# The gate projection of an encoder layer: a fourth block of 768 columns in seven products, and another order at the end

## The chip, the cores and the metric

The kernel runs on one core of one Trainium2 chip. The metric is the device time of one execution in microseconds (us); the median of several runs is compared. A profile is one execution recorded by the hardware profiler. In it PE is TensorE (matmuls), PEld its weight loads, DVE is VectorE, ACT is ScalarE, POOL is GpSimd, and SP is the engine whose queue issues most DMAs.

## The reference

One encoder layer over 256 tokens (two row blocks of 128) with a model width of 4096, in float32. The part that matters here is its end, after the output projection has been added to the residual `x`:

```
x = x + concat([y_a, y_b]) @ w_out
ple  = p @ w_ple                                         # (256, 256) @ (256, 4096)
gate = sigmoid(rms_norm(x, g_ple) @ w_ple_gate)          # (256, 4096) @ (4096, 4096)
x = x + ple * gate
return rms_norm(x, g_final)
```

The rest (input projection, latent attention, dilated attention, output projection) is the same in both kernels.

## The kernel before, in words

**Matmuls in three parts.** Each float32 operand is split into a high and a low part: ACT copies `hi` in a shorter format (L115), DVE subtracts `lo = src - hi` (L116). A product is then three matmuls, hi x hi, hi x lo and lo x hi, into one PSUM bank (`mm`, L130 to L135). The left operand, 128 tokens of one row tile of 128 inner indices, is the stationary one; 256, 384, 400 or 512 weight columns stream. So the weights must be loaded and split anew for every row tile, which is the steady work of SP, ACT and DVE.

**Steps.** All weight work is a list `steps`, run in order at the end of the function (L1465 to L1503). At step i the program issues loads ahead (`fetch`, at most RAW = 4 raw tiles held), then splits ahead (`convert`, into a ring of tiles: three `wp` tiles, in the wide blocks a fourth, `B4`), then the matmuls of step i, then one round of `advance`, which lets each spawned task (a Python generator) issue its next few instructions up to its `yield`. Every engine works through its own instructions in the order in which the program issued them; semaphores order the engines among one another. The last 25 steps look further ahead.

**Seven products (class `Block`, L769).** A wide block covers 1024 columns, as two halves, for both row blocks. Two row tiles (a pair j of 16), two row blocks and two column halves make a 2 x 2 x 2 product of blocks. A plain step (`plain_step`) does one row tile as 4 products, 12 matmuls; a pair is 8 products. A fast pair (`fast_steps`) does it in seven: four steps with 1, 2, 2 and 2 products, 21 matmuls. It needs four subtractions on DVE for the weights (L820) and sums of the left operand, which `x1_sums` has made once for pairs 0 to 6 (`zs`, in the slots B0, B2, B3, B7a and B5). `weave(fast, lead, trail, 2)` writes out the order: `lead` plain steps, then fast pairs with plain steps between, then `trail` plain steps with the two embedding steps (`wide_ple`) after the second of them. `wide_mid` (L1013) combines the products after the last fast step, `wide_done` (L1025) adds the rest after the last step, applies tanh (for the sigmoid), multiplies by the embedding, adds to the residual tile `x1[c]` and takes the squares for the final norm.

**The gate projection before.** Three wide blocks (k = 0, 1, 2) cover columns 0 to 3071, with 6, 7 and 7 fast pairs. Then come plain chunks (`Chunk`, `Old` steps): columns 3072 to 3583 (c = 6, 512 wide), 3584 to 3839 (c = 7, 256 wide) and 3840 to 4095 (c = 8, 256 wide). The last is done first for row block 0 over all 32 row tiles (eight steps of four row tiles), then for row block 1 with the same split weights, which are kept (`kept`, `stay`; five of the eight steps have slots of their own, the other three stay in the ring). So row block 0 can be finished while PE still works for row block 1. `done_g` (L1073) finishes a chunk; for c = 8 it goes on into `finish(t)` (L1113): the inverse root by three Newton steps, then for each of eight column tiles a scale and an output DMA from SP.

**g_final before.** `load_g` (L969) starts two steps after the last wide block and loads one of eight pieces of 512 columns per step, from SP, into B2 and B3. `late_gains` (L1106) multiplies the finished tiles 0 to 5 by it on DVE, `done_g` does so for columns 3072 to 3839, so the last scales are plain `tensor_scalar` (DVE) or a scaled copy (ACT, every third), except for the last 256 columns.

Of the kernel before, what the change touches and what calls it, by code (L numbers as in the profile page):

```python
# [66 lines left out]
class Chunk:  # L67
# [4 lines left out]
    def __init__(self, src, nk, n, lhs, banks, done, needs=lambda j: (), per=2, ts=(0, 1), keep=None):  # L72
        self.src, self.nk, self.n, self.lhs, self.banks = src, nk, n, lhs, banks
        self.done, self.needs, self.per, self.ts, self.keep = done, needs, per, ts, keep
        self.ps = None
# [3 lines left out]
def encoder_layer(ctx: ExitStack, tc: tile.TileContext, x, p, positions, g_mix, w_in, g_q_latent, w_uq,  # L79
# [625 lines left out]
    ss1, ss2 = (stat(NT * n).rearrange("p (t c) -> p t c", t=NT) for n in (8, 9))  # L705
# [52 lines left out]
    class Step:  # L758
# [4 lines left out]
        def __init__(self, load, split, run, needs=(), frees=0):  # L763
            self.load, self.split, self.run, self.needs, self.frees, self.after = load, split, run, needs, frees, None
            self.ring, self.flag = WP, None
# [3 lines left out]
    class Block:  # L769
# [9 lines left out]
        def __init__(self, w, lhs, sums, name, order, needs, tags, tmp, ring):  # L779
            self.w, self.lhs, self.sums, self.name, self.needs, self.tmp = w, lhs, sums, name, needs, tmp  # L780
            self.ring, self.tags = ring, dict(zip(self.NAMES, tags))
            self.ps, self.left = {}, {}
            for kind, _ in order[0]:
                for m in ("M1", "M5", "M7", "M6", "M4", "M2", "M3") if kind == "fast" else ("M2", "X", "M3", "M4"):
                    self.left[m] = self.left.get(m, 0) + 1

        def product(self, m, a, b):
            first = m not in self.ps
            if first:
                self.ps[m] = bank(self.tags[m], [Q])  # L790
            self.left[m] -= 1
            mm(self.ps[m], a, b, first, self.left[m] == 0)

        def load(self, kt):
            r = wp.tile([P, 2, Q], F32, tag="raw", name=f"raw_{kt}", bufs=RAW)
# [16 lines left out]
        def fast_steps(self, j):  # L812
# [9 lines left out]
            def split1(hi, lo):  # L822
                if isinstance(self.tmp, tuple):
                    T.extend(slot(b, [2, Q]) for b in self.tmp)
                else:
                    both = slot(self.tmp, [4, Q])
# [113 lines left out]
    blocks = [(512 * c, 512) for c in range(7)] + [(3584, 256), (3840, 256)]  # L940
    FAST, WIDE = 7, 3
# [27 lines left out]
    def load_g():  # L969
        for i in range(2):  # L970
            gF.append(slot(f"B{2 + i}", [2048]))
            for n in range(0, 2048, 512):
                nc.sync.dma_start(gF[i][:, n:n + 512],
                                  g_final[2048 * i + n:2048 * i + n + 512].unsqueeze(0).to_broadcast([P, 512]))
                if i == 1 and n == 0:
                    spawn(late_gains())
                yield

    P4 = {}
    WIDE_PLE = {(0, 0): "m0", (0, 1): "m1", (1, 0): "t0", (1, 1): "t1"}  # L980

    def wide_ple(k):
# [3 lines left out]
        def step(kt):  # L986
            box = []

            def load():
                box.append(wp.tile([P, 2, Q], F32, tag="raw", name=f"raw_e{kt}", bufs=RAW))  # L990
                nc.sync.dma_start(box[0].rearrange("p a b -> p (a b)"),
                                  w_ple[kt * P:(kt + 1) * P, 1024 * k:1024 * (k + 1)])

            def run(hi, lo):
                for (t, h), tag in WIDE_PLE.items():
                    if kt == 0:
                        ps[t, h] = bank(tag, [Q])
# [5 lines left out]
            return Step(load, lambda hi, lo: split(hi, lo, box[0]), run, ["pT", ("mid", k)], 1)  # L1003

        def out():
            for at in WIDE_PLE:
                nc.scalar.activation(P4[at], ps[at], AF.Copy)
# [5 lines left out]
    def wide_mid(k, blk):  # L1013

        def task():
            e = blk.e = slot("B1", [4, Q])
# [8 lines left out]
    def wide_done(k, blk):  # L1025
        def task():
# [5 lines left out]
            for n in range(6):  # L1032
                for i, t, h, m in quarters[n:n + 1]:
                    nc.scalar.activation(e[:, i], e[:, i], AF.Tanh, scale=r1h[:, t:t + 1])
                for i, t, h, m in quarters[n - 1:n] if n else ():
                    u, xc = e[:, i], x1[2 * k + h][:, t]
                    nc.vector.scalar_tensor_tensor(u, u, 1.0, P4[t, h], op0=ALU.add, op1=ALU.mult)
                    nc.vector.tensor_tensor(xc, u, xc, op=ALU.add)
                for i, t, h, m in quarters[n - 2:n - 1] if n > 1 else ():
                    xc = x1[2 * k + h][:, t]  # L1040
                    nc.scalar.activation(e[:, i], xc, AF.Square, accum_out=ss2[:, t, 2 * k + h:2 * k + h + 1])
                yield
        return task
# [23 lines left out]
    def x_cols(lo, n, t):  # L1067
        return x1[lo // 512][:, t, lo % 512:lo % 512 + n]

    def g_cols(lo, n):  # L1070
        return gF[lo // 2048][:, lo % 2048:lo % 2048 + n]

    def done_g(c, ts=(0, 1)):  # L1073
        lo, n = blocks[c]

        def task(ps):
            if not U:
                U.extend([slot("Q0", [512]), junk])
            for t in ts:
                nc.scalar.activation(U[t][:, :n], ps[t], AF.Tanh, scale=r1h[:, t:t + 1])  # L1080
            if c < 8:
                yield
            for t in ts:
                u, xc = U[t][:, :n], x_cols(lo, n, t)
                nc.vector.scalar_tensor_tensor(u, u, 1.0, ple[c][t], op0=ALU.add, op1=ALU.mult)
                nc.vector.tensor_tensor(xc, u, xc, op=ALU.add)
            if c < 8:
                yield
            for t in ts:
                u, xc = U[t][:, :n], x_cols(lo, n, t)  # L1090
                if c < 8:
                    nc.scalar.activation(u, xc, AF.Square, accum_out=ss2[:, t, c:c + 1])
                    nc.vector.tensor_tensor(xc, xc, g_cols(lo, n), op=ALU.mult)
                else:
                    nc.vector.scalar_tensor_tensor(u, xc, 1.0, xc, op0=ALU.mult, op1=ALU.mult,
                                                   accum_out=ss2[:, t, 8:9])
            if c == 7:
                yield
                for t in range(NT):
                    nc.vector.tensor_reduce(part2[t], ss2[:, t, :8], axis=AX.X, op=ALU.add)  # L1100
                    nc.vector.tensor_scalar(part2[t], part2[t], 1.0 / DM, EPS, op0=ALU.mult, op1=ALU.add)
            if c == 8:
                yield from finish(ts[0])
        return task

    def late_gains():  # L1106
        for c in range(2 * WIDE):
            for t in range(NT):
                nc.vector.tensor_tensor(x1[c][:, t], x1[c][:, t], g_cols(512 * c, 512), op=ALU.mult)
                yield  # L1110
                yield

    def finish(t):  # L1113
        r, a, h, w = r2[:, t:t + 1], stat(1), stat(1), stat(1)
        nc.vector.tensor_scalar(a, ss2[:, t, 8:9], 1.0 / DM, part2[t], op0=ALU.mult, op1=ALU.add)
# [9 lines left out]
        for c in range(8):  # L1125
            xc = x1[c][:, t]
            if c == 7:
                nc.vector.tensor_scalar(xc[:, :256], xc[:, :256], r, None, op0=ALU.mult)
                nc.vector.scalar_tensor_tensor(xc[:, 256:], xc[:, 256:], r, g_cols(3840, 256), op0=ALU.mult,
                                               op1=ALU.mult)  # L1130
            elif c % 3 == 1:
                nc.scalar.activation(xc, xc, AF.Copy, scale=r)
            else:
                nc.vector.tensor_scalar(xc, xc, r, None, op0=ALU.mult)
            nc.sync.dma_start(out[t * P:(t + 1) * P, 512 * c:512 * (c + 1)], xc)
            if t == 0:
# [43 lines left out]
    def lay(blk, order, mid, done, ple=None, after=(), used={}):  # L1180
# [5 lines left out]
        for i, key in enumerate(shape):  # L1186
            x = next(step[key])
            x.ring = WP + list(after) if after != () and i > last else blk.ring
# [100 lines left out]
    kept = [("B1",), ("B4",), ("B5",), ("B6",), ("B7a", "T6")]  # L1289
    stay = []  # L1290

    def embed(c, lo, n, tags):
        return Chunk(cols(w_ple, lo, n), 2, n, lambda kt: (pT[0][:, 0, kt], pT[0][:, 1, kt]), tags, done_p(c),
                     lambda j: ["pT"])

    for k in range(WIDE):
        order = weave(*((range(6), 6, 4) if k == 0 else (range(7), 4, 4)), 2)
        blk = Block(w_ple_gate[:, 1024 * k:1024 * (k + 1)], lhs_x1, x1_s, "x1_sums", order,
                    lambda kt: [("x1T", kt // 4)], LAST, "B6", WP + ["B4"])
        lay(blk, order, wide_mid(k, blk), wide_done(k, blk), wide_ple(k))  # L1300
    wide_end = len(steps)
    hooks[wide_end + 2] = lambda: spawn(load_g())
    tail_banks = {6: (("m0", "m1"), ("t0", "t1")), 7: (("m2", "o"), ("s", "m3")), 8: (("m0", "m1"), ("t0", "t1"))}

    for c, (lo, n) in enumerate(blocks):
        if c < 2 * WIDE:
            continue
        w, per = cols(w_ple_gate, lo, n), 1024 // n
        small = embed(c, lo, n, tail_banks[c][1])

        def gate(done, **k):
            return Chunk(w, 32, n, lhs_x1, tail_banks[c][0], done,
                         lambda j, per=per: [("x1T", kt // 4) for kt in range(per * j, per * (j + 1))], per=per, **k)

        if c < 8:
            g = gate(done_g(c))
            half = 12 // per
            add(g, 0, half)
            add(small)
            add(g, half)  # L1320
        else:
            add(small)
            for t in range(NT):
                add(gate(done_g(c, (t,)), ts=(t,), keep=(stay, t == 0)))
# [4 lines left out]
    class Old(Step):  # L1329


        def __init__(self, i, ch, j):
            self.i, self.ch, self.j, self.ring = i, ch, j, WP
            self.needs, self.after, self.flag = ch.needs(j), None, None
            kept_before = ch.keep and not ch.keep[1]
            self.load = None if kept_before else self.fetch
            self.frees = 0 if kept_before else 1
# [189 lines left out]
```

## Time and profile before

| What | us |
|---|---|
| Runs shown (3) | 1927.67, 1927.89, 1929.81; median 1927.89 |
| Profiled execution | 1927.64 |
| Its span, first to last instruction | 1925.9 |
| PE busy | 1909.8 (99%) |
| DVE busy | 1560.8 (81%) |
| ACT busy | 1101.3 (57%) |
| POOL busy | 74.5 (4%) |
| Last matmul ends, from the span's start | 1913.63 |

The difference between the execution and its span (1.7 us) lies around the recorded instructions. Times inside the profile count from the span's start. Matmuls overlap: a matmul's own duration is longer than the distance to the next, so prices are taken from starts. In tile names of the profile numbers are left out: `m` is any of the banks m0 to m3, `B` any of several slots, `Ah` and `Al` the high and low parts of the left operand.

### The profile page before, as it was taken

What the parts mean: (1) busy time and instruction counts of PE and PEld (TensorE: products, weight loads), DVE (VectorE), ACT (ScalarE), POOL (GpSimd) and SP (SyncE); (2) the same over time, 40 slices, a digit from 0 to 9 for tenths busy, and PEclk for the clock granted to TensorE, in tenths of its full rate; (3) what the DMA queues carried; (4) which work ended last, traced back from release to release, by engine and by line L of the source; (5) the groups of instructions that cost most, each with busy time, mean ns of one, the idle gap of its engine ahead of it and who ended that gap; (6) DMA issues with size and microseconds to landing.
All of it is one profiled execution on the core that took longest, in us unless ns stands there. A gap on an engine that the chain in (4) does not pass through costs nothing.

```text
span 1925.9 us, 25586 instructions
## 1 busy us (share of the span) xinstructions
PE 1909.8 (99%) x9272; PEld 1626.7 (84%) x9272; DVE 1560.8 (81%) x2162; ACT 1101.3 (57%) x1513; POOL 74.5 (4%) x122
## 2 busy tenths in 40 slices
PE   9999999999999999999999999999999999999997
PEld 8998889998888888888888888888888888888887
DVE  7766966665999999999887778889896698989866
ACT  6555555565555555655556666555565456666643
POOL 1001011220000000000000010000000000000000
PEclk9999999999999999999999999999999999999999
DMA  7676655455666666666664456665666656566675
GB/s 251 188 187 198 196 172 144 145 150 162 188 185 209 209 217 197 209 197 196 218 197 139 135 165 218 201 215 174 230 194 217 189 184 218 186 210 204 207 220 176
DMA packets 147342, 370.59 MB, mean 192 GB/s; under 512 B 12020, under 2 KB 45904, under 8 KB 147216
## 3 DMA queue, kind: packets, MB, share of 16 engines
q1 hardware_dynamic: 145584, 363.90, 61.9%
q0 software_dynamic: 1632, 5.05, 0.7%
q8 instruction: 73, 1.20, 0.3%
q14 instruction: 53, 0.43, 0.1%
HBM read 364.72 MB, written 4.19 MB: 192 GB/s over the span
## 4 chain that ended last, share of the span: by engine, by line
PE 94%; DVE 4%; DMA 1%; issue 1%; ACT 1%; SPq 0%; DVEq 0%; ACTq 0%
PE m L134 20%; PE m L135 20%; PE m L133 20%; PE t L134 4%; PE t L135 4%; PE t L133 4%; PE s L134 3%; PE o L134 3%; PE o L135 3%; PE o L133 3%; PE s L135 3%; PE s L133 3%; DVE lo L116 1%; PE t L445 1%; DVE B L820 1%
## 5 line engine op out<-in xcount | busy, mean ns | idle before, releaser
L116 DVE TENSOR_TENSOR lo<-raw,hi 128x1024 fp32r<-128x1024 f32 (+4 forms) x497 | 549.0, 1109 | 227.6 <-ACT hi L115 225.0
L115 ACT ACTIVATE hi<-raw 128x1024 fp32r<-128x1024 f32 (+4 forms) x497 | 478.4, 967 | 365.9 <-PE m L135 181.2
L133 PE MATMUL m<-hi,Ah 128*128 128x512 f32 (+2 forms) x1130 | 429.2, 380 | 0.0
L134 PE MATMUL m<-lo,Ah 128*128 128x512 f32 (+2 forms) x1130 | 424.6, 376 | 0.9 <-DVE lo L116 0.7
L135 PE MATMUL m<-hi,Al 128*128 128x512 f32 (+2 forms) x1128 | 422.3, 374 | 0.0
L134 PEld LDWEIGHTS m<-lo,Ah 128*128 128x128 f32 x1130 | 212.9, 188 | 34.6 <-DVE lo L116 5.0
L135 PEld LDWEIGHTS m<-hi,Al 128*128 128x128 f32 x1128 | 212.3, 188 | 32.8 <-DVE Al L127 0.2
L133 PEld LDWEIGHTS m<-hi,Ah 128*128 128x128 f32 x1130 | 213.0, 188 | 30.1
L133 PE MATMUL m<-hi,B 128*128 128x512 f32 (+1 forms) x420 | 160.4, 382 | 0.0
L134 PE MATMUL m<-lo,B 128*128 128x512 f32 (+1 forms) x420 | 156.8, 373 | 0.2 <-DVE lo L116 0.2
L135 PE MATMUL m<-hi,B 128*128 128x512 f32 (+1 forms) x420 | 156.7, 373 | 0.0
L115 ACT ACTIVATE hi<-B 128x1024 fp32r<-128x1024 f32 x75 | 79.5, 1061 | 79.9 <-DVE B L820 50.3
L116 DVE TENSOR_TENSOR lo<-B,hi 128x1024 fp32r<-128x1024 f32 x75 | 91.6, 1223 | 4.1 <-ACT hi L115 1.8
L135 PEld LDWEIGHTS m<-hi,B 128*128 128x128 f32 x420 | 78.9, 188 | 11.7
L134 PEld LDWEIGHTS m<-lo,B 128*128 128x128 f32 x420 | 79.1, 188 | 11.3 <-DVE lo L116 0.9
L133 PEld LDWEIGHTS m<-hi,B 128*128 128x128 f32 x420 | 79.0, 188 | 10.6
L115 ACT ACTIVATE B<-raw 128x1024 fp32r<-128x1024 f32 (+1 forms) x66 | 60.5, 925 | 45.8 <-DMA raw<-in_w_in_dram 17.4
L820 DVE TENSOR_TENSOR B<-raw,B 128x512 f32<-128x512 f32 x126 | 86.3, 685 | 0.0
L115 ACT ACTIVATE B<-B 128x1024 fp32r<-128x1024 f32 (+1 forms) x60 | 57.4, 957 | 44.4 <-DVE B L820 22.1
L116 DVE TENSOR_TENSOR B<-raw,B 128x1024 fp32r<-128x1024 f32 (+1 forms) x66 | 69.4, 1059 | 13.5 <-ACT B L115 13.2
L116 DVE TENSOR_TENSOR T<-t,T 128x512 fp32r<-128x512 f32 (+1 forms) x65 | 44.4, 683 | 41.6 <-ACT T L115 41.2
L835 DVE TENSOR_TENSOR lo<-raw,hi 128x1024 fp32r<-128x1024 f32 x57 | 69.5, 1219 | 1.9 <-ACT hi L833 1.8
(780 smaller groups left out, 3774.3 us busy)
## 6 DMA issues: line engine op xcount, KB each, us to landing
raw<-in_w_in_dram SPq DMA_DIRECT2D x320, 512.0 KB, 4.1
raw<-in_w_out_dram SPq DMA_DIRECT2D x128, 512.0 KB, 4.4
raw<-in_w_ple_gate_dram SPq DMA_DIRECT2D x128, 512.0 KB, 4.4
raw<-in_w_in_dram SPq DMA_DIRECT2D x63, 400.0 KB, 3.7
raw<-in_w_uq_dram SPq DMA_DIRECT2D x32, 384.0 KB, 3.5
raw<-in_w_ukv_dram SPq DMA_DIRECT2D x16, 512.0 KB, 3.7
T<-in_x_dram SPq DMA_DIRECT2D x7, 512.0 KB, 6.0
T<-in_x_dram POOLq DMA_DIRECT2D x7, 512.0 KB, 8.2
```

Of the source, the lines that this page charges most:

```text
L115: nc.scalar.activation(hi, src, AF.Copy)
L116: nc.vector.tensor_tensor(lo, src, plain(hi), op=ALU.subtract)
L133: nc.tensor.matmul(ps, ah, bh, start=start, stop=False)
L134: nc.tensor.matmul(ps, ah, bl, start=False, stop=False)
L135: nc.tensor.matmul(ps, al, bh, start=False, stop=stop)
L445: nc.tensor.transpose(tp[:, k, t * P:(t + 1) * P], e[:, t, k * P:(k + 1) * P], ident)
L820: nc.vector.tensor_tensor(dst, a, b, op=ALU.subtract)
L835: nc.vector.tensor_tensor(lo, r[1], plain(hi), op=ALU.subtract)
```

## The change

Four things are done together, all of them after block 2.

1. Columns 3072 to 3839 become a fourth wide block (k = 3) with halves of 384 columns (`q`), six fast pairs in the order 1, 2, 3, 4, 0, 5 with 6 plain steps ahead and 6 behind. After its last fast step its ring is the three `wp` tiles only. Its halves cross the borders of the 512-column tiles, so `wide_done` works in pieces.
2. The last 256 columns: weight steps 0 to 3 run for row block 0 alone, steps 4 to 7 for both row blocks (row block 0 first within a step), then 0 to 3 for row block 1 with kept weights (`KEPT`, four slots).
3. g_final is multiplied in the last scale (`scalar_tensor_tensor` on DVE) for six of the eight tiles; tiles 1 and 4 (`EARLY`) are multiplied ahead of it by GpSimd and scaled by ACT. `late_gains` is gone.
4. The loads of g_final start when the fourth fast pair of block 3 has used its sums in B2 and B3 (`z used`), one per step.

```
-    FAST, WIDE = 7, 3
+    FAST, WIDE = 7, 4
...
     def load_g():
+        while "z used" not in flags:
+            yield
         for i in range(2):
             gF.append(slot(f"B{2 + i}", [2048]))
-            for n in range(0, 2048, 512):
-                nc.sync.dma_start(gF[i][:, n:n + 512], ...)
-                if i == 1 and n == 0:
-                    spawn(late_gains())
-                yield
+        for c in (1, 4, 0, 2, 3, 5, 6, 7):
+            g = g_cols(512 * c)
+            nc.sync.dma_start(g, g_final[512 * c:512 * (c + 1)].unsqueeze(0).to_broadcast([P, 512]))
+            yield
+            if c in EARLY:
+                for t in range(NT):
+                    nc.gpsimd.tensor_tensor(x1[c][:, t], x1[c][:, t], g, op=ALU.mult)
...
+    def done_last(t, ps):
+        def task():
+            u, xc = U[t][:, :256], x1[7][:, t, 256:]
+            nc.scalar.activation(u, ps[t], AF.Tanh, scale=r1h[:, t:t + 1])
+            nc.vector.scalar_tensor_tensor(u, u, 1.0, ple[8][t], op0=ALU.add, op1=ALU.mult)
+            nc.vector.tensor_tensor(xc, u, xc, op=ALU.add)
+            nc.vector.scalar_tensor_tensor(u, xc, 1.0, xc, op0=ALU.mult, op1=ALU.mult, accum_out=ss2[:, t, 9:10])
+            yield from finish(t)
...
     def finish(t):
...
         for c in range(8):
             xc = x1[c][:, t]
-            if c == 7:
-                nc.vector.tensor_scalar(xc[:, :256], xc[:, :256], r, None, op0=ALU.mult)
-                nc.vector.scalar_tensor_tensor(xc[:, 256:], xc[:, 256:], r, g_cols(3840, 256), ...)
-            elif c % 3 == 1:
+            if c in EARLY:
                 nc.scalar.activation(xc, xc, AF.Copy, scale=r)
             else:
-                nc.vector.tensor_scalar(xc, xc, r, None, op0=ALU.mult)
+                nc.vector.scalar_tensor_tensor(xc, xc, r, g_cols(512 * c), op0=ALU.mult, op1=ALU.mult)
             nc.sync.dma_start(out[t * P:(t + 1) * P, 512 * c:512 * (c + 1)], xc)
-            if t == 0:
+            if t == 0 and c % 2:
                 yield
...
     for k in range(WIDE):
-        order = weave(*((range(6), 6, 4) if k == 0 else (range(7), 4, 4)), 2)
+        q = Q if k < 3 else 384
+        order = weave(*((range(6), 6, 4), (range(7), 4, 4), (range(7), 4, 4), ((1, 2, 3, 4, 0, 5), 6, 6))[k], 2)
...
+        if k == 3:
+            hook(len(steps), lambda: spawn(load_g()))
+        lay(..., **({"after": [], "used": {4: "z used"}} if k == 3 else {}))
+    small = Chunk(cols(w_ple, 3840, 256), 2, 256, ..., ("t0", "t1"), done_p(8), lambda j: ["pT"])
+    steps.insert(len(steps) - 2, (small, 0))
+    KEPT, PER = ("B5", "B6", "B4", "B0"), 4
...
+        def run(hi, lo):
+            for t in ts:
+                for k in range(PER):
+                    left[t] -= 1
+                    a = tuple(q[:, t * P:(t + 1) * P] for q in lhs_x1(PER * j + k))
+                    mm(last_ps[t], a, (hi[:, k], lo[:, k]), left[t] == DM // P - 1, left[t] == 0)
...
+    n = DM // P // PER
+    steps += [last_step(j, (0,) if j < len(KEPT) else (0, 1), 1) for j in range(n)]
+    steps[-1].after = done_last(0, last_ps)
+    steps += [last_step(j, (1,), 0) for j in range(len(KEPT))]
+    steps[-1].after = done_last(1, last_ps)
```

More of the change, by code (lines that the diff above doesn't have):

```diff
@@ L1065, in done_p, with g_cols @@
         return task
[L1067 to L1076, printed above, removed]
+    def g_cols(lo):
+        return gF[lo // 2048][:, lo % 2048:lo % 2048 + 512]
+    def done_last(t, ps):
+        def task():
+            assert "part2" in flags
             if not U:
                 U.extend([slot("Q0", [512]), junk])
[L1079 to L1096, printed above, removed]
-            if c == 7:
[L1098 to L1103, printed above, removed]
-        return task
@@ L1334, in __init__ @@
             self.needs, self.after, self.flag = ch.needs(j), None, None
-            kept_before = ch.keep and not ch.keep[1]
-            self.load = None if kept_before else self.fetch
-            self.frees = 0 if kept_before else 1
-            self.own = kept_before or ch.keep and j < len(kept)
+            self.load, self.frees, self.shape = self.fetch, 1, [ch.per, ch.n]
         def fetch(self):
```

158 lines of the change are left out of this document (73 added, 85 removed).

## The prediction

> **What bounds the kernel now.** I read the page first: busy time by engine and the chain that ended last.
>
> ```profile
> PE 1909.8 (99%) x9272; PEld 1626.7 (84%) x9272; DVE 1560.8 (81%) x2162; ACT 1101.3 (57%) x1513; POOL 74.5 (4%) x122
> ...
> PE 94%; DVE 4%; DMA 1%; issue 1%; ACT 1%; SPq 0%; DVEq 0%; ACTq 0%
> ```
>
> TensorE carries 94% of the chain, so a change pays where it removes matmul time, or where it shortens what comes after the last matmul. Next the windows over the part that changes (columns: length; busy time of PE, PEld, DVE, ACT, POOL; granted clock; DMA share; GB/s).
>
> ```profile
> 1800.00:1820.00 20.00, 20.00 (x90) 16.53 (x90) 13.66 (x17) 10.81 (x14) 0.00 (x0) 1.00 0.56 184
> 1822.00:1824.00 2.00, 2.00 (x10) 1.66 (x9) 1.96 (x3) 1.00 (x2) 0.00 (x0) 1.00 0.98 354
> 1832.00:1834.00 2.00, 2.00 (x10) 1.69 (x9) 1.80 (x2) 1.48 (x3) 0.00 (x0) 1.00 0.95 256
> 1900.00:1926.00 26.00, 13.62 (x112) 13.23 (x110) 12.48 (x44) 3.62 (x6) 0.00 (x0) 0.86 0.42 162
> ```
>
> PE is full from the end of block 2 (about 1818.2) to the last matmul, and DMA is saturated where g_final is read beside the weights. The timeline of PE gives the price of a matmul, as the distance between starts, since matmuls overlap:
>
> ```profile
> 422.64 0.34 PE L133 MATMUL m<-hi,B 128*128 128x384 f32 x1
> ...
> 424.55 0.33 PE L135 MATMUL m<-hi,B 128*128 128x384 f32 x1
> ...
> 1863.96 0.39 PE L135 MATMUL m<-hi,Al 128*128 128x512 f32 x1
> 1864.19 0.28 PE L133 MATMUL m<-hi,Ah 128*128 128x256 f32 x1
> ...
> 1900.27 0.28 PE L133 MATMUL m<-hi,Ah 128*128 128x256 f32 x1
> 1900.53 0.39 PE L134 MATMUL m<-lo,Ah 128*128 128x256 f32 x1
> ```
>
> Eleven distances over 1.91 us make 0.1736 us for 384 columns; over longer runs of starts I read 0.2268 for 512 and 0.1200 for 256. The jump at 1900.27 is a short stall. The chain of waits gives the end: the last matmul ends at 1913.63, the span at 1925.9.
>
> ```profile
> 1913.72 0.48 ACT junk L1080
> ...
> 1917.58 0.49 DVE T L1134
> ```
>
> These end rows are row block 1: tanh, sum of squares, Newton steps, then eight scales and eight output DMAs. The span is 1925.9 us, the execution 1927.64, the median of the runs 1927.89. I take differences on the execution and add them to the median. A difference of 0.2%, 3.86 us, is about what a measurement of this kernel can tell from no change.
>
> **Matmuls of columns 3072 to 3839.** Before: 192 gate and 12 embedding matmuls of 512 columns, as many of 256: 204 x 0.2268 + 204 x 0.1200 = 70.75 us. After: ten plain pairs are 20 row tiles x 12 = 240, six fast pairs 6 x 21 = 126, the embedding 24: 390 of 384 columns, 390 x 0.1736 = 67.70 us. All on the path: **-3.05 us**. Eighteen matmuls go for six products, and the fixed part of each matmul's price shrinks, for 0.1200 is more than half of 0.2268. The sums of A come from the existing x1_sums, so nothing is added there.
>
> **The last 256 columns.** 204 matmuls of 256 before and after. Before, row block 0 alone runs through all eight weight steps, one every 12 x 0.12 = 1.44 us, and its 96 matmuls take 11.84 us from 1890.10 to 1901.94 instead of 11.52. Now only four steps have that pace, the other four serve both row blocks at 2.88 us, and a split costs DVE 1.14. I take the stall as gone: **-0.32 us**. Bounds 0 and -0.32.
>
> **The tail.** Row block 0's last matmul now lies (12 + 48) x 0.12 = 7.2 us ahead of the last one, E. Before it was 11.5 us. Its chain to the scales takes 1917.58 - 1913.63 = 3.95 us, so its scales start at E - 3.25. Six of them are now scalar_tensor_tensor on DVE. Starts of that form with a pointer scalar lie 0.66 apart (657.66 and 658.32): 6 x 0.66 = 3.96, and DVE is free at E + 0.71. Behind them on DVE stands row block 1's chain, which could start at E + 0.59 (1914.22 - 1913.63), and behind that the last eight output DMAs: +0.12. Row block 1's first scale takes 0.74 instead of 0.49, so its first DMA goes 0.25 later. After that SP issues one per 0.5 us in either kernel (1918.09 to 1921.59 for eight), slower than the scales come (six on DVE, two on ACT). Tail **+0.37 us**. If row block 0's chain waited for the whole last shared step, 12 matmuls longer, it would be 1.8.
>
> **g_final in the last scale.** Twelve late multiplications and two more groups leave DVE: no gain, since DVE has gaps of 1.5 us there. Four multiplications go to GpSimd, whose queue is empty at the end. The eight loads of g_final move from gaps of 2.7 us to the steps after the fourth fast pair, one per step: 8 x 0.26 MB = 2.1 MB within pair 5 and two steps of pair 6, 0.52 + 2.08 + 3 x 1.04 + 2.08 + 0.52 = 8.3 us. On SP the weight loads of pair 6 and of the trail are queued behind them. Weights need (4 + 3) x 0.39 MB in 13.5 us, 1.7 MB in 8.3. Together 3.8 MB; at 302 GB/s, the mean of the saturated windows from 1822 to 1840, this takes 12.6 us, 4.3 late. Four raw tiles are fetched ahead: 4/7 of 13.5 = 7.7 us, less 3.5 for a 384 KB load to land, covers 4.2. I take **+0.2 us**; at the slowest window, 256 GB/s, it is 2.3, and 0 if all hides. SP's wait until B3's sums are read costs nothing: its next load waits for a later step anyway.
>
> **Vector work of block 3.** Starts give 0.605 us for 512 elements (1789.83, 1790.43) and 1.14 for 1024, so by a line 0.47 for 384 and 0.87 for 768. After the fourth pair, to the last fast step, PE has 2 x 21 + 3 x 12 matmuls, 13.5 us; DVE has ten short operations and nine long ones, 12.5. The spare is 1.0 us, and two converted steps ahead in the ring add 2.1. Into this stretch fall the four GpSimd multiplications of 512 elements, by 0.46 us for 128 and 0.74 for 256 about 1.30 each. What they do to DVE is seen once (the timeline of both):
>
> ```profile
> 160.99 0.31 POOL L213 TENSOR_TENSOR T<-T,ss 128x64 f32<-128x64 f32 x1
> ...
> 161.25 1.41 DVE L116 TENSOR_TENSOR lo<-raw,hi 128x1024 fp32r<-128x1024 f32 x1 [1.54 <-ACT hi L115]
> 161.27 0.31 POOL L214 TENSOR_TENSOR T<-T,ss 128x64 f32<-128x64 f32 x1
> ...
> 161.66 1.61 POOL L215 TENSOR_TENSOR T<-T,T 128x256 f32<-128x256 f32 x1
> ```
>
> The split takes 1.41 instead of 1.23, and the next GpSimd operation more than twice its 0.74. So each holds up the other, DVE by less than the GpSimd work in its way. If DVE stood still for all four: 4 x 1.30 = 5.2, less the cover of 3.1, leaves PE a stall of 2.1 us; the other bound is 0. I take the middle, **+1.1 us**, since this row shows about half a block.
> The Trainium skill, page "SBUF — State Buffer", section "Who interferes with whom", speaks against the change: a VectorE instruction with two SBUF inputs and a GpSimd instruction that reads SBUF exclude each other, and the second waits for the whole of the first. By that rule the stall is the upper bound; the row agrees in kind, not in full size.
>
> **Sum.** -3.05 - 0.32 + 0.37 + 0.2 + 1.1 = **-1.7 us**: 1925.9 for the execution, 1926.2 on the median. Its own range is -3.0 (nothing stalls) to +1.4 (both bounds): 1924.9 to 1929.3.
>
> **Rivals.**
> *Full exclusion.* The row above shows a wait in both directions; each GpSimd operation then stops DVE for all its 1.30 us. For it: DVE is nearly without gaps there. Against it: 1.41 is not 1.23 + 0.62. It gives -3.0 + 0.2 + 2.1 = -0.7, 1927.2; a chance of 0.2, within no difference.
> *Cheaper columns.* If 384 columns cost three quarters of 512, 0.170 us, and nothing stalls: 390 x 0.0035 = 1.4 more, -4.4, 1923.5. Against it: twelve starts in a row show 0.1736. With the scatter of the runs (1927.67 to 1929.81) I give faster by over 0.2% a chance of 0.2.
> *GpSimd stretched, DVE held with it (slower).* The longest 256-element operation on GpSimd took 1.545 us, 3.1 for 512: four take 12.4, less 3.1 of cover is a stall of 9.3 in pairs 5 and 6. -3.0 + 0.2 + 9.3 = +6.5, 1934.4. It decides from about 2.4 us held each. For it: DVE is fuller there than where those rows come from. Against it: the longest rows were themselves the waiting side. Chance 0.15.
> *The products save nothing.* This would need PE to wait in block 3 as much as it saves; blocks 1 and 2, with the same scheme, lose 0.3 us each (39.65 and 39.72 of 40 us busy). It lies inside the no-difference case, 1927.9.
>
> **Numbers.** The likeliest case, full exclusion and no saving lie within 0.2%: 0.65 together. Faster 0.2, slower 0.15. The range takes in the cheaper columns and half of the way into the slow rival: 1923.4 to 1930.8.
>
> **What would show it.** Right: 366 gate and 24 embedding matmuls of 384 columns 0.174 apart; PE's end near 1910.3 plus stalls of 1 to 2 us in pairs 5 and 6, with DVE splits longer than 0.96 beside the GpSimd operations; row block 1's first DVE operation about 0.7 us after the last matmul, and 12.6 us from the last matmul to the end of the span. Wrong: PE waits at the last eight weight steps, or splits that wait for DMA after the fourth pair, or a stall of over 3 us.

## The result: 3.4 us slower, and the profile after

The changed kernel takes 1930.89 us, median of 21 runs (1929.43 to 1933.64); before, run beside it, 1927.45, median of 21 (1926.14 to 1929.81). The ratio is 1.0018, 95% interval 1.0013 to 1.0024. The forecast was 1926.2, range 1923.4 to 1930.8: the change made the kernel slower instead of faster, and the median lies 0.1 us above the upper end of the range. A second set gave 1931.57 against 1927.66 (experiment 1).

The profiled execution after took 1929.53, span 1927.6: 1.9 above the one of before. Its page, busy times and the shares of the chain that ended last:

```profile
PE 1907.9 (99%) x9254; PEld 1630.7 (85%) x9254; DVE 1580.6 (82%) x2198; ACT 1112.3 (58%) x1542; POOL 81.2 (4%) x126
...
PE 90%; DVE 7%; DMA 1%; ACT 1%; issue 1%; SPq 0%; DVEq 0%; ACTq 0%
```

The 18 matmuls are gone (9272 to 9254) and PE is busy 1.9 us less, yet the end is later: PE now waits, and DVE's share of the chain went from 4% to 7%. The waits of PE after, over the whole kernel, say for what (total us, times, longest):

```profile
PE m L134 <- DVE lo L116: 2.3, 8, 0.6
...
PE m L134 <- DVE lo L839: 1.1, 1, 1.1
PE m L134 <- DVE B L116: 1.1, 1, 1.1
```

L839 is a split inside a fast pair, and the two single waits of 1.1 us end at 1868.4 and 1870.9, in block 3. The windows after, in the columns of before (length; PE, PEld, DVE, ACT, POOL; clock; DMA share; GB/s), show where:

```profile
1862.00:1864.00 2.00, 2.00 (x13) 2.00 (x12) 1.30 (x2) 1.84 (x3) 1.23 (x1) 1.00 0.92 178
1864.00:1866.00 2.00, 1.42 (x8) 1.10 (x8) 2.00 (x2) 0.58 (x1) 2.00 (x3) 1.00 0.98 307
1866.00:1868.00 2.00, 1.31 (x8) 0.99 (x6) 2.00 (x2) 0.00 (x0) 2.00 (x3) 1.00 1.02 394
1868.00:1870.00 2.00, 1.32 (x6) 1.00 (x6) 2.00 (x3) 0.00 (x0) 1.52 (x1) 1.00 0.90 354
1870.00:1872.00 2.00, 1.14 (x6) 1.06 (x7) 1.88 (x3) 1.94 (x3) 0.00 (x0) 1.00 0.57 125
...
1896.00:1898.00 2.00, 1.46 (x12) 1.25 (x11) 2.00 (x3) 1.22 (x3) 0.00 (x0) 1.00 0.93 288
```

From 1864 to 1872 PE does a third less than it could. DVE is full there, and so is POOL until 1869.5. The timeline of DVE there, and then that of POOL:

```profile
1862.95 1.92 DVE L116 TENSOR_TENSOR lo<-raw,hi 128x768 fp32r<-128x768 f32 x1 [0.70 <-ACT hi L115]
1864.80 1.63 DVE L824 TENSOR_TENSOR B<-raw,B 128x384 f32<-128x384 f32 x1
1866.35 2.03 DVE L839 TENSOR_TENSOR lo<-raw,hi 128x768 fp32r<-128x768 f32 x1
1868.30 1.64 DVE L824 TENSOR_TENSOR B<-raw,B 128x384 f32<-128x384 f32 x1
1869.86 0.94 DVE L116 TENSOR_TENSOR B<-B,B 128x768 fp32r<-128x768 f32 x1
```

```profile
1862.77 6.75 POOL L983 TENSOR_TENSOR T<-T,B 128x512 f32<-128x512 f32 x4 [406.28 <-DMA B<-in_g_final_dram]
```

The same DVE rows in the kernel without the multiplications (experiment 2):

```profile
1863.11 0.96 DVE L116 TENSOR_TENSOR lo<-raw,hi 128x768 fp32r<-128x768 f32 x1 [0.66 <-ACT hi L115]
1863.99 0.55 DVE L824 TENSOR_TENSOR B<-raw,B 128x384 f32<-128x384 f32 x1
1864.46 0.95 DVE L839 TENSOR_TENSOR lo<-raw,hi 128x768 fp32r<-128x768 f32 x1
1865.33 0.55 DVE L824 TENSOR_TENSOR B<-raw,B 128x384 f32<-128x384 f32 x1
1865.79 0.95 DVE L116 TENSOR_TENSOR B<-B,B 128x768 fp32r<-128x768 f32 x1
```

Four DVE operations in a row are longer by 0.96, 1.08, 1.08 and 1.09 us, 4.2 in all, and the fifth, when GpSimd is done, is as long as ever. GpSimd and DVE go in turn, each DVE operation behind one GpSimd multiplication: in the trace the four multiplications start at 1862.77, 1864.02, 1865.98 and 1867.53 and take 1.29, 1.99, 1.58 and 2.00 us, so the later three wait for DVE as well.

One thing more stands in the first row: DVE was idle for 0.70 us just before it, waiting for ACT, and ACT had waited 1.94 us for the load of that weight tile.

**The balance of the two profiles.** I count as lost what lies between two starts of PE beyond 0.1736 us (384 columns) or 0.1200 (256). Block 3 and the last columns take 97.3 us after, from 1817.50 to 1914.83 (the last start and 0.12): 67.70 + 24.48 of matmuls and 5.15 lost. Of that 0.67 lies in the third and fourth fast pair (1849.8 to 1856.3), 3.65 in the next two beside GpSimd, 0.81 at 1896.74. Before lost 0.29 in all from there on. So: -3.05 + 4.86, the tail +0.34 (12.60 against 12.26 from the end of the last matmul to the end of the span), -0.45 ahead of block 3, which starts at 1817.50 instead of 1817.95, and +0.2 around the span: +1.9. The -0.45 lies ahead of block 3 and is taken as scatter. The tail after, in the chain in order of time (start, length, engine, output, line):

```profile
1915.09 0.66 DVE T L1125
1915.75 0.34 DVE junk L1102
...
1919.02 0.75 DVE T L1125
```

Row block 1's first DVE operation (L1102) waits behind the last of six scales of row block 0 and starts 0.76 us after the last matmul, which ends at 1914.99. Its own first scale starts at 1919.02.

### The profile page after: what moved, and what is told of

It reads as the page before. It is cut to its first block, busy times and chain, and to the rows that moved or that the text cites. A ratio compares the mean times of both kernels' runs of the same rounds, so it can differ in the third digit from the quotient of the medians.

```text
span 1927.6 us, 25662 instructions
## 1 busy us (share of the span) xinstructions
PE 1907.9 (99%) x9254; PEld 1630.7 (85%) x9254; DVE 1580.6 (82%) x2198; ACT 1112.3 (58%) x1542; POOL 81.2 (4%) x126
## 4 chain that ended last, share of the span: by engine, by line
PE 90%; DVE 7%; DMA 1%; ACT 1%; issue 1%; SPq 0%; DVEq 0%; ACTq 0%
PE m L134 19%; PE m L135 19%; PE m L133 19%; PE t L133 4%; PE t L135 4%; PE t L134 3%; PE s L134 3%; PE s L133 3%; PE s L135 3%; PE o L134 3%; PE o L135 3%; PE o L133 3%; DVE lo L116 2%; DVE B L824 1%; DMA raw<-in_w_ple_gate_dram 1%
## 5 line engine op out<-in xcount | busy, mean ns | idle before, releaser
L133 PE MATMUL m<-hi,Ah 128*128 128x512 f32 (+3 forms) x1080 | 409.9, 380 | 0.1
L134 PE MATMUL m<-lo,Ah 128*128 128x512 f32 (+3 forms) x1080 | 405.7, 376 | 3.3 <-DVE lo L116 2.1
L135 PE MATMUL m<-hi,Al 128*128 128x512 f32 (+3 forms) x1078 | 403.0, 374 | 0.0
L115 ACT ACTIVATE hi<-B 128x1024 fp32r<-128x1024 f32 (+1 forms) x85 | 87.9, 1035 | 92.3 <-DVE B L824 59.9
L116 DVE TENSOR_TENSOR lo<-B,hi 128x1024 fp32r<-128x1024 f32 (+1 forms) x85 | 101.0, 1190 | 5.0 <-ACT hi L115 2.1
L824 DVE TENSOR_TENSOR B<-raw,B 128x512 f32<-128x512 f32 (+1 forms) x138 | 94.9, 687 | 0.0
L115 ACT ACTIVATE B<-raw 128x1024 fp32r<-128x1024 f32 (+2 forms) x68 | 61.4, 910 | 47.7 <-DMA raw<-in_w_in_dram 20.0
L115 ACT ACTIVATE B<-B 128x1024 fp32r<-128x1024 f32 (+2 forms) x62 | 59.1, 954 | 43.3 <-DVE B L824 23.7
L116 DVE TENSOR_TENSOR B<-raw,B 128x1024 fp32r<-128x1024 f32 (+2 forms) x68 | 70.2, 1039 | 13.3 <-ACT B L115 13.0
L839 DVE TENSOR_TENSOR lo<-raw,hi 128x1024 fp32r<-128x1024 f32 (+1 forms) x61 | 74.3, 1218 | 2.7 <-ACT hi L837 2.7
```

Of the source, the lines that this page charges most:

```text
L115: nc.scalar.activation(hi, src, AF.Copy)
L116: nc.vector.tensor_tensor(lo, src, plain(hi), op=ALU.subtract)
L133: nc.tensor.matmul(ps, ah, bh, start=start, stop=False)
L134: nc.tensor.matmul(ps, ah, bl, start=False, stop=False)
L135: nc.tensor.matmul(ps, al, bh, start=False, stop=stop)
L824: nc.vector.tensor_tensor(dst, a, b, op=ALU.subtract)
```

## The experiments

Theory **exclusion**: GpSimd's multiplications hold up DVE, which is full there, and PE waits for its splits. Rival **burst**: the eight loads of g_final make the weights late. Rival **VectorE too full**: block 3's fast pairs cost DVE more than PE anyway. Before, run beside each group, had medians of 1927.07 to 1927.69. Lost times are those of the profiled execution.

**1. The changed kernel again.**

> The changed kernel itself once more, beside the next three. Two accounts of why its median (1930.89) lies further above before (+3.4 us) than its profiled execution does (+1.9). A: the stalls in pairs 5 and 6 (3.65 us in the profile) now and then set off a stretch at half clock, as in the kernels with longer stalls; then the runs spread over some 3 us, and the mean clock of a run falls with its time (0.998 near 1929, 0.996 near 1932), and this profile may show a stretch of 0.50. B: the 1.5 us are scatter of the upstream work; then the same spread as before has (some 2.5 us), with no such tie. Either way a median of 1930.3 to 1931.5.

1931.57 (1929.33 to 1932.87), ratio 1.0019 (1.001 to 1.0028). Its profile, 1929.47, lost 5.1 us again: 0.67 in the third and fourth pair, 3.1 beside GpSimd, 1.24 in the last 256 columns. It shows no stretch at half clock. The weight tile came earlier here: ACT waited 1.41 us for it instead of 1.94, DVE 0.17 instead of 0.70, and PE lost 0.5 less beside GpSimd.

**2. How much the multiplications cost: none, two, four, eight.**

```
             if c in EARLY:
-                for t in range(NT):                    # none
+                for t in (0, 1, 0, 1):                 # eight
+                for t in range(NT if c == 1 else 0):   # two
```

> The changed kernel without the four GpSimd multiplications of tiles 1 and 4 by g_final (those tiles come out without that gain); the loads of g_final stay. Exclusion (each GpSimd multiplication keeps the split on DVE waiting for its whole 1.08 us): the 3.65 us that PE loses from 1864 to 1871 fall to under 0.5, and the time to about that of the kernel before (-0.3 us, range -1.5 to +0.8). Burst (the eight loads of g_final delay the weights): the loss stays at 2 us or more, and the time stays 2 to 3.5 us above before. Vector load (DVE is too full there, whatever is added): as exclusion here.

> The changed kernel with the two GpSimd multiplications of tile 1 alone (tile 4 goes out without g_final). None gave 1926.95, four 1930.9 to 1931.6, eight 1933.45. If each multiplication holds VectorE for its own time (1.08 us a piece in the trace) behind a fixed cover, two hold it 2.2 us: PE's stall in pairs 5 and 6 is 1.0 to 1.6 us instead of 3.65, the time 1928 to 1929. If it is the mere presence of GpSimd work there (a queue, a semaphore), two cost nearly as much as four: above 1930.

> The changed kernel with each of the four GpSimd multiplications done twice (tiles 1 and 4 get the gain squared). Exclusion: eight instead of four splits or subtractions are 1.08 us longer, four of them in the trail, where DVE has gaps of 1.1 us per 2.08: PE loses another 1 to 4 us, the time is 5 to 8 us above before. Burst: nothing changes, +3.4 us. Vector load: as exclusion, or a little less.

| Multiplications | us (median) | ratio to before, 95% | PE lost beside them |
|---|---|---|---|
| none | 1926.95 | 0.9999 (0.999 to 1.0008) | 0.3, late weights |
| two | 1927.72 | 1.0002 (0.9994 to 1.0011) | 1.3 |
| four | 1930.89, 1931.57 | 1.0018 (1.0013 to 1.0024), 1.0019 (1.001 to 1.0028) | 3.65, 3.1 |
| eight | 1933.45 | 1.0032 (1.002 to 1.0045) | 4.5, and 3.0 at half clock |

The kernels with none and two leave g_final out of tiles 1 and 4 or of tile 4; the one with eight multiplies it in twice. All loads are kept with none, and the loss falls from 3.65 to 0.3: exclusion, not burst. That kernel still loses 1.43 us in the last 256 columns (experiment 5). The four multiplications cost PE 2.9 to 3.4 us in the profiles and 3.9 to 4.6 by the medians; the difference belongs to what stays open below. The first two cost less, as they would if a small cover is used up first. With eight something else comes in; the windows of that kernel:

```profile
1872.00:1874.00 2.00, 0.00 (x0) 0.00 (x0) 2.00 (x3) 1.78 (x3) 2.00 (x2) 0.88 0.62 160
1874.00:1876.00 2.00, 1.90 (x6) 1.78 (x6) 2.00 (x3) 0.91 (x2) 2.00 (x2) 0.50 0.90 253
1876.00:1878.00 2.00, 2.00 (x8) 1.78 (x6) 2.00 (x3) 0.00 (x0) 2.00 (x2) 0.50 0.02 5
```

In a gap of 2.3 us, behind two shorter ones, the granted clock falls to 0.50, and matmuls of 384 columns start 0.32 us apart instead of 0.1736.

**3. The multiplications on VectorE, at the same place.**

```
-                    nc.gpsimd.tensor_tensor(x1[c][:, t], x1[c][:, t], g, op=ALU.mult)
+                    nc.vector.tensor_tensor(x1[c][:, t], x1[c][:, t], g, op=ALU.mult)
```

> The changed kernel with the four multiplications on DVE at the same place in the program, instead of on GpSimd. They take 4 x 0.605 = 2.4 us of DVE instead of the 4.2 us by which GpSimd lengthened its operations, but DVE then waits in its order for g_final to land. Exclusion: a loss of 1.5 to 2.5 us in place of 3.65 if g has landed by then, time 1 to 2.5 us above before; if DVE has to wait for g, up to 4 us more. Burst: +3.4 us or more. Vector load: about +3 us.

1932.58, ratio 1.0028 (1.0019 to 1.0038). This does not weigh the work alone: DVE waited 3.58 us for the piece of g_final, with the splits of the next steps queued behind, so PE stood still once for 4.15 us and then had 3.4 us at half clock. GpSimd's own queue had kept that wait off DVE.

**4. The multiplications after the last fast pair.** Pieces 1 and 4 are loaded last, once `wide_mid` of block 3 has been issued.

```
-        for c in (1, 4, 0, 2, 3, 5, 6, 7):
+        for c in (0, 2, 3, 5, 6, 7, 1, 4):
+            while c in EARLY and ("mid", 3) not in flags:
+                yield
```

> The changed kernel with pieces 1 and 4 of g_final loaded last, after the last fast step, so that the four GpSimd multiplications fall into the plain steps behind it. Exclusion: the lengthened DVE operations lie where DVE has 1.1 us to spare per step, PE loses under 0.8 us in pairs 5 and 6 and none by them in the trail; time -0.3 us against before (-1.5 to +0.8). Burst: six of the eight loads stay where they are, so about three quarters of the loss stays, +2.5 us. Vector load: as exclusion.

1928.51, ratio 1.0007 (0.9998 to 1.0016): 2.4 to 3 us of the cost are gone, though the time is 0.4 above the range expected. Left are 0.74 in pairs 3 and 4, 0.65 at 1863.9 where ACT waited 2.73 us for a weight tile (six loads of g_final are bunched there), and 1.25 at the fifth weight step of the last 256 columns.

**5. What makes PE wait at that fifth step.** First the four additions of `wide_done` one step later:

```
             quarters = ((0, 0, 0, "M2"), (3, 1, 1, "X"), (1, 0, 1, "M3"), (2, 1, 0, "M4"))
+            if k == 3:
+                yield
             for i, t, h, m in quarters:
```

> Pieces 1 and 4 of g_final with their GpSimd multiplications after the last fast pair (as in the third of the first runs, 1928.5), and now also the four additions of block 3's end on VectorE one step later, behind the split of the first shared weight step of the last 256 columns. If the additions make PE wait there (1.25 us in that run): the stall falls to 0.4 or less, about 1927.6. If the late weights do (ScalarE waited 1.64 us on that DMA): the stall stays at 1 us and the time at 1928.5.

1929.47, ratio 1.001 (1.0001 to 1.0019). The stall stayed at 1.24, and a new one of 0.9 came at the last weight step, to which DVE's later work had moved. The timeline of ACT in that kernel says what the step waited for:

```profile
1893.25 1.06 ACT L115 ACTIVATE hi<-raw_l 128x1024 fp32r<-128x1024 f32 x1 [2.04 <-DMA raw_l<-in_w_ple_gate_dram]
```

So the weights are late. Four steps for row block 0 alone want four 512 KB tiles in 5.8 us (4 x 1.44). Then the steps in turn, one for row block 0 alone, one for both:

```
-            if j < len(KEPT):
+            if j % 2 == 0:
                 if new:
-                    both = slot(KEPT[j], [2, PER, 256], F32R)
+                    both = slot(KEPT[j // 2], [2, PER, 256], F32R)
...
-    steps += [last_step(j, (0,) if j < len(KEPT) else (0, 1), 1) for j in range(n)]
+    steps += [last_step(j, (0,) if j % 2 == 0 else (0, 1), 1) for j in range(n)]
...
-    steps += [last_step(j, (1,), 0) for j in range(len(KEPT))]
+    steps += [last_step(2 * j, (1,), 0) for j in range(len(KEPT))]
```

> The changed kernel without the four multiplications (tiles 1 and 4 go out without g_final; 1926.95 in an earlier run, PE stalled 1.4 us at the fifth weight step of the last 256 columns), and with the weight steps of the last 256 columns in turn for row block 0 alone and for both, instead of four of the one kind and then four of the other. In the second order four 512 KB tiles are wanted within 5.8 us (364 GB/s), in turn they are wanted at 243 GB/s on average. If late weights make that stall (the additions moved away from it left it at 1.14 us): it falls to 0.3 or less and the time to about 1925.6, 1.9 below before. If it is VectorE's work of block 3's end: it stays, 1927.

> The whole computation, with both remedies: pieces 1 and 4 of g_final and their GpSimd multiplications after the last fast pair (1928.51 by themselves, stall of 1.25 us at the fifth weight step of the last 256 columns), and those weight steps in turn. If late weights make the stall: 1927.4, as fast as before or a little faster. If not, or if the multiplications now hold up the splits of the last weight steps: 1928.5 or more.

Without multiplications: 1926.18, ratio 0.9993 (0.9984 to 1.0002). With them after the last fast pair: 1927.30, ratio 1.0 (0.9991 to 1.0009). The stall is gone in both, as the windows of the first show:

```profile
1894.00:1896.00 2.00, 2.00 (x19) 2.00 (x18) 1.54 (x2) 2.00 (x4) 0.00 (x0) 1.00 0.82 251
1896.00:1898.00 2.00, 2.00 (x19) 2.00 (x18) 1.92 (x3) 1.60 (x4) 0.00 (x0) 1.00 0.08 25
```

**6. More plain steps between the fast pairs.** Both kernels carry the late pieces of experiment 4 and the later additions of experiment 5.

```
-((1, 2, 3, 4, 0, 5), 6, 6))[k]
+((1, 2, 3, 4, 0, 5), 4, 6))[k]
```

> As the one before, and ten plain steps instead of eight between the fast pairs of block 3 (four instead of six ahead of them). From the rows a fast pair and one plain step take VectorE 6.16 us (1847.69 to 1853.85) and PE 33 x 0.1736 = 5.73; with two plain steps 7.03 and 7.81. If VectorE is the bound in pairs 3 and 4 (stalls of 0.67 us there): they go, at most 0.2 us left, about 0.5 us off the time. If weights come late there: no change.

The second kernel has that too. It loads g_final more slowly, and three of the six other pieces (5, 6 and 7) behind pieces 1 and 4, after the last fast pair:

```
-        for c in (0, 2, 3, 5, 6, 7, 1, 4):
+        for c in (0, 2, 3, 1, 4, 5, 6, 7):
...
             yield
+            if c not in EARLY:
+                yield
```

> As the one before, with six of the eight loads of g_final in every second step instead of every step (pieces 1 and 4, which GpSimd multiplies, one step each after the last fast pair as before). If the burst of g_final makes the weights late after the fourth fast pair (ScalarE waited 2.73 us on a weight tile there, PE 0.65): that stall goes and the time falls by about 0.5 us, to 1926.5, with all stalls of PE from block 3 to the end below 1 us. If it doesn't, the time is that of the one before. All of block 3's stalls gone would be 1924.9 (the lower end of the prediction's own range).

1931.40 and 1930.99, ratios 1.0022 (1.0012 to 1.0032) and 1.0019 (1.001 to 1.0028). In the third and fourth pair 0.2 and 0.36 us were lost instead of 0.7 to 0.9: VectorE had been the bound there. But the first pair now meets DVE's work at the end of block 2 (2.0 us lost at 1830 to 1834 in both), the last weight step lost 1.6 and 1.2, and two steps before it 0.8 and 1.2 together. The slower and later loads halved the stall after the fourth pair (0.94 to 0.46). The expected gain was turned into new waits.

**7. The multiplications at a place where VectorE has gaps.** All three have the last weight steps in turn and a piece of g_final every second step. In the first, pieces 1 and 4 are loaded first, and only the issue of the multiplications is put behind the last fast pair:

```
+        spawn(early_g())
         for c in (1, 4, 0, 2, 3, 5, 6, 7):
...
+            nc.sync.dma_start(g_cols(512 * c), ...)
+            yield
+            yield
...
+    def early_g():
+        while ("mid", 3) not in flags:
+            yield
+        for c in EARLY:
+            for t in range(NT):
+                nc.gpsimd.tensor_tensor(x1[c][:, t], x1[c][:, t], g_cols(512 * c), op=ALU.mult)
+            yield
```

> The whole computation, with the weight steps of the last 256 columns in turn (as in the kernel that took 1927.30), the eight loads of g_final in every second step from the fourth fast pair on, pieces 1 and 4 first, and the GpSimd multiplications from the end of the last fast pair on (about 1876 to 1884), one tile a step, where VectorE is idle a third to a half of the time. There 2.58 us of PE were lost: 0.6 in pairs 3 and 4, 0.25 at 1871, 0.87 at 1874 where the embedding weights came late behind the burst of g_final, 0.80 at 1884 beside GpSimd. If burst and exclusion make the last three, they fall to 0.6 in all and the time to about 1926.0 (1.1 below before, 5 below the changed kernel). If GpSimd's four holds of 1.08 us cannot be hidden there either, the stall is 1 to 2 us beside them and the time 1927 to 1928. If the embedding weights are late for another reason, the 0.87 stays.

1930.43, ratio 1.0011 (1.0002 to 1.002). They did not move: GpSimd began at 1863.14, as soon as its piece had landed, since its queue was empty and nothing but the data holds it. PE lost 3.7 us there, as in the changed kernel, with the loads spread out: against the burst once more. ACT still waited for the weight tile ahead of the first held split, 2.02 us. The embedding weights' 0.87 was gone.

In the second, pieces 1 and 4 are loaded fifth and sixth, so that the data come later; the third is the same without the multiplications:

```
-        for c in (1, 4, 0, 2, 3, 5, 6, 7):
+        for c in (0, 2, 3, 5, 1, 4, 6, 7):
...
             if c in EARLY:
                 for t in range(NT):
                     nc.gpsimd.tensor_tensor(x1[c][:, t], x1[c][:, t], g, op=ALU.mult)
+            yield
```

> The whole computation; as the last run, but pieces 1 and 4 of g_final are the fifth and sixth that are loaded, one every second step, so that the GpSimd multiplications cannot start before about 1874. If their cost is VectorE's fullness beside them, most of the 3.66 us of stall goes and 0.5 to 1.5 us is left between 1874 and 1886; the time falls from 1930.43 to 1926.5 to 1927.5. If four multiplications cost PE 3.7 us wherever they stand, it stays near 1930.

> The same kernel without the four GpSimd multiplications (tiles 1 and 4 go out without g_final), all loads as in it. What the multiplications cost at their new place is the difference of the two: 0 to 1 us if VectorE's gaps hide them, 3.7 to 4 if not. By the rows PE should lose no more than 0.7 us here (pairs 3 and 4), and the time should be 1925.5, which is the prediction's sum without a stall (-3.05 + 0.37 + 0.3) from 1927.5.

With: 1926.31 (1925.11 to 1927.72), ratio 0.9994 (0.9985 to 1.0003). Without: 1925.68, ratio 0.9991 (0.9982 to 1.0). By the medians the multiplications cost 0.6 us here, where they had cost 3.9 to 4.6. The timeline of POOL in the kernel with them, then that of DVE, then its windows, and last DVE in the kernel without them:

```profile
1871.69 7.18 POOL L983 TENSOR_TENSOR T<-T,B 128x512 f32<-128x512 f32 x4 [415.49 <-DMA B<-in_g_final_dram]
```

```profile
1872.16 3.60 DVE L116 TENSOR_TENSOR lo<-raw_e,hi 128x768 fp32r<-128x768 f32 x2
1875.69 4.61 DVE L116 TENSOR_TENSOR lo<-raw,hi 128x768 fp32r<-128x768 f32 x3
```

```profile
1872.00:1874.00 2.00, 2.00 (x13) 2.00 (x12) 2.00 (x3) 0.85 (x1) 2.00 (x2) 1.00 0.90 338
1874.00:1876.00 2.00, 2.00 (x13) 2.00 (x13) 2.00 (x2) 0.85 (x1) 2.00 (x2) 1.00 0.55 175
```

```profile
1872.21 1.82 DVE L116 TENSOR_TENSOR lo<-raw_e,hi 128x768 fp32r<-128x768 f32 x2
1875.12 0.96 DVE L116 TENSOR_TENSOR lo<-raw,hi 128x768 fp32r<-128x768 f32 x1 [1.09 <-ACT hi L115]
1877.20 0.96 DVE L116 TENSOR_TENSOR lo<-raw,hi 128x768 fp32r<-128x768 f32 x1 [1.12 <-ACT hi L115]
1879.06 0.69 DVE L116 TENSOR_TENSOR lo<-raw,hi 128x512 fp32r<-128x512 f32 x1 [0.91 <-ACT hi L115]
1881.36 0.96 DVE L116 TENSOR_TENSOR lo<-raw,hi 128x768 fp32r<-128x768 f32 x1 [1.60 <-ACT hi L115]
```

DVE is held almost as long as before: the five splits of the two DVE rows take 1.63, 2.05, 2.04, 2.04 and 0.68 us instead of 0.95, 0.95, 0.96, 0.96 and 0.69, 3.9 in all. But in the third kernel DVE has gaps of 1.09, 1.12, 0.91 and 1.60 us between these splits, and the holds fall into them: the split that starts at 1881.36 there starts at 1881.50 here. PE loses nothing beside them.

They are still not free. SP issues the next load of a raw tile only when DVE has read it, so the first weight load of the last 256 columns goes out at 1879.72 instead of 1878.18, ACT waits for late weights, and DVE's work for the end of block 3 comes later. In this profile row block 0's last chain then holds up that of row block 1: from the last matmul to the end of the span it takes 13.93 us, without the multiplications 12.61. This execution, 1927.21, is the second slowest of its set; by the medians the price is smaller.

This kernel computes the whole reference; its median is 1.1 us below before and 4.6 to 5.3 below the changed kernel. The interval against before reaches just past 1, so it is not shown to be faster than before.

## Why the prediction was wrong, step by step

- **Matmuls of columns 3072 to 3839, -3.05.** Right: starts 0.1736 apart, 390 of them, and block 3 to the last matmul is 92.2 us plus what was lost.
- **Vector work of block 3, +1.1. This step failed.** It lost 3.65 us beside GpSimd (3.1 in the second profile) and 0.67 in the pairs before, over the upper bound of 2.1. The hold was 4.2 us, inside the 5.2 that this bound assumed. The cover was wrong: 3.1 was assumed (1.0 of spare and 2.1 in the ring), 0.6 was there, 1.1 in the second profile. The spare had been averaged to the last fast step, and the ring counted as full. But a fast pair and one plain step cost DVE 6.16 us (1847.69 to 1853.85) and PE 5.73, so in pairs 3 and 4 DVE is itself the bound, and the 0.67 us lost there show that the ring was empty. It was empty again when GpSimd began: of the 0.96 us by which the first split was held, PE lost 0.85 at once. A late weight tile took a part of the cover, the 0.70 us for which DVE stood idle just before (0.17 in the second profile).
- **The row read as half a block.** One split 0.18 longer beside two operations of 64 elements, 0.31 us each, was taken for the size of the effect; operations that short cannot hold a split for long. The last row of the same fence had the full size in the other direction: that GpSimd operation took 1.61 us instead of 0.74, 0.87 longer, so its own 0.74 began at 162.53, about where the split ended (162.66). In block 3 every DVE operation with two SBUF inputs behind a multiplication was held for 0.96 to 1.09 us, of the 1.29 that the first multiplication took. The Trainium skill, page "SBUF — State Buffer", section "Who interferes with whom", says so: the second waits for the whole of the first. The four rows above agree, nearly in full size, and taking the middle against that rule was an error.
- **Full exclusion**, the rival at 0.2, had the right mechanism, with that same cover: -0.7 instead of the measured result. **GpSimd stretched**, the slower rival at 0.15, had the right sign and place, but DVE was held 1.08 each and not the 2.4 from which it was to decide; it was the cover that decided.
- **The last 256 columns, -0.32. Wrong in sign: +0.5** (0.81 lost instead of 0.34; 1.24 in the second profile). The pace of 1.44 us a step was said to matter less over four steps; but those come one behind the other, each wants 512 KB, and the loads took 4.9 us to land (median) with four raw tiles held. In turn, the stall is gone.
- **g_final, burst +0.2.** Too small, but near: with the loads and without the multiplications 0.3 us was lost at 1869 and 0.4 at 1873, far from the bound of 2.3. The late weight tile of the step above comes on top.
- **The tail, +0.37.** Right: +0.34, by the steps named, the first scale 4.03 us after the last matmul instead of 3.95, and 0.75 instead of 0.49 long.
- **The terms that were right add up.** The profile of the last kernel of experiment 7 ends 2.1 us before that of before: -3.05 for the matmuls, +0.35 for the tail, +0.6 for what PE still loses, mostly in pairs 3 to 5. Its median lies 1.7 below before. That 1.7 is also the forecast for the changed kernel is chance: the forecast had +1.1 for multiplications that this kernel leaves out.
- **The signs.** Of what the prediction named as signs of being wrong, all three came: a stall of over 3 us, PE's wait at the last eight weight steps, and a split after the fourth pair that waited, through ACT, for a load. The two bounds of the sum ended at 1929.3; the range reached to 1930.8 only by the slow rival.

**What stays open.** The profiles of the changed kernel lie 1.9 us above that of before, the medians 3.4 and 3.9. So 1.5 to 2 us of the median, and with it the step past the end of the range, have no shown cause. Each profiled execution is the second fastest of its set, so what the slower ones do is not seen. Its 32 runs had mean granted clocks of 0.998 (7 runs, mean 1930.3), 0.997 (15, 1931.2) and 0.996 (10, 1931.4); of 119 runs of before beside the experiments 5 had 0.996. One stretch at half clock after the stalls in some runs would do this, as in experiments 2 and 3. No profile of the changed kernel caught one, so it is not shown. Another part lies outside the recorded span: 2.2 to 3.2 us in 8 of the 32 runs, 1.7 to 1.9 in all of before.

## What to carry to other kernels

A GpSimd multiplication of two SBUF operands beside a full VectorE cost VectorE about its whole running time here (1.08 of 1.29 us). It cost TensorE nothing only where VectorE had gaps of that size, and those are read from the stage itself, pair by pair, not from an average over it. Even there the held splits freed their tiles late. GpSimd, with an empty queue, started when its data landed, although its instructions were issued after the last fast pair: to move such work, move its data. Before a ring of converted tiles is counted as cover, look whether the steps ahead have already emptied it.

## What the runs showed of the hardware

- Four multiplications of 128x512 took GpSimd 6.75 us beside VectorE, in turn with VectorE's operations, which were each 0.96 to 1.09 us longer. In the second kernel of experiment 5 that takes the steps in turn, two took 2.54 us while VectorE stood idle (1880.56 to 1883.10), and the next two 3.26 beside two splits that took 3.98 together instead of 1.82.
- A short gap of TensorE can halve the clock: about the end of single gaps of 2.3 us (behind two shorter ones) and of 4.15 us the granted clock fell to 0.50, for 6.8 and 3.4 us, with matmuls of 384 columns 0.32 us apart instead of 0.1736. After the gaps of 0.9, 1.4 and 1.4 us of the changed kernel its profile shows none. The Trainium skill, page "TensorE: Matmul & The Clock Gate", section "Part 1: The HAM clock gate", gives a free-running window of about 3.4 us, of which one that is idle brings half the clock; the 3.4 us and twice that agree with it, but a gap of 2.3 us is shorter than a whole window, and the clock fell all the same.
